# Transposed projections emitted in pieces of 12 matrix products instead of 6, in a two-layer hybrid attention encoder

## The chip, the cores and the metric

One Trainium2 chip, one core of it. The number is device time in microseconds (us) of one execution of the whole program, the median of several. Five engines of the core take part: PE (matrix products and transposes), DVE and POOL (elementwise), ACT (activation functions), SP (which here only issues DMAs). Each has its own list of instructions and goes through it in order; they meet through semaphores.

## The reference

Two layers over x of 512 positions by 1024 channels, float32. Each layer normalises x, multiplies it by one wide input matrix (1024 by 6152), runs three kinds of attention on the result, gates them, multiplies by one output matrix, normalises and adds:

```python
h = rms_norm(x, g_pre)
p = h @ w_in
qa, ka, va, ga, qs, ks, vs, gs, qf, kf, vf, gf, ff = jnp.split(p, split_at, axis=-1)
...
ya = diff_attention(qa, ka, va, lam, lambda_init, subln) * silu(ga)    # "a": 4 heads, two score maps each
yb = stick_breaking_attention(qs, ks, vs) * silu(gs)                    # "b": 8 heads
yc = forgetting_attention(qf, kf, vf, cum_log_f) * silu(gf)             # "c": 8 heads
y = jnp.concatenate([ya, yb, yc], axis=-1) @ w_out
return x + rms_norm(y, g_post)
```

(Reshapes between heads and channels are left out of this excerpt.) All three attentions are causal, and are taken in four blocks of 128 query positions; block i sees (i + 1) * 128 keys.

## The kernel before, in words

Full precision is made of three products: each operand is split in a high part and a rest (`hl`, `hT`), and `mm3` issues high by high (L192), high by rest (L193) and rest by high (L194) into one PSUM sum. A weight unit of 256 columns arrives by DMA, ACT copies its high part (L176) and POOL subtracts for the rest (L182).

There are two kinds of projections. `proj_N` makes v, with positions on the partitions. `proj_T` makes q, k and the gates transposed: 128 channels on the partitions, all 512 positions along the row, so that one projection is 8 chunks of the inner dimension times 3 products of 128x512, 24 in all. A layer has 36 of them (24 for q and k, 12 for the gates), the program 72.

Attention is woven between the projections by a list that the program sorts by a planned time. `do(cost, fn)` puts a piece of a projection on the main list and moves the planned clock `now` on by `cost`; `at(t, fn)` puts an operation of attention, or a copy out of PSUM, on the side list at a time t. In the end both lists are sorted together and emitted in that order. A piece of a projection is not divided: a side operation whose time falls within a piece is emitted behind it. The groups go a, c, b; the attention of a group runs while the next group's projections are on PE, and the attention of b while the gates are.

One step of attention (one head or one half of a pair, one block i) is a chain: scores on PE (L339, two products per score tile `s`), softmax pieces on DVE and ACT (L364 adds the mask and finds the minimum `mn`, L373 exponentiates, L464 and L466 normalise; in b, ACT takes two sigmoids at L499 and L500, and DVE scans and multiplies at L506 and L511), transposes on PE into `pt` (L347), a copy out of PSUM (L350 on ACT or L352 on DVE), and the product with v on PE (`ov`, L399 in a, L437 in b and c). The score tiles have two PSUM buffers, `pt` two, `ov` one, the projections `pj` three.

Of the kernel before, what the change touches and what calls it, by code (L numbers as in the profile page):

```python
# [60 lines left out]
def hybrid_kernel(ctx, tc, x, w_in, forget_bias, diff_lambda, diff_subln, w_out, pre_norm, post_norm, consts, out):  # L61
# [72 lines left out]
    def do(cost, fn):  # L134
        main.append((now[0], 1, len(main), fn))
        now[0] += cost

    def at(t, fn):
        side.append((t, 0, len(side), fn))
# [51 lines left out]
    def mm3(ps, lh, ll, rh, rl, first, last):  # L191
        nc.tensor.matmul(out=ps, lhsT=lh, rhs=rh, start=first, stop=False)  # L192
        nc.tensor.matmul(out=ps, lhsT=lh, rhs=rl, start=False, stop=False)  # L193
        nc.tensor.matmul(out=ps, lhsT=ll, rhs=rh, start=False, stop=last)  # L194

    def proj_T(k0, c, hT, done):

        st = {}

        def go(q):  # L200
            if q == 0:
                st["ps"] = pj_p.tile([128, S], F32, name="pj", tag="pj")
            for kc in range(2 * q, 2 * q + 2):
                w = halves[k0 + kc // 4]["hl"][:, :, kc % 4, c * 128:(c + 1) * 128]
                h = hT()
                mm3(st["ps"], w[:, 0], w[:, 1], h[0][:, kc], h[1][:, kc], kc == 0, kc == KC - 1)

        for q in range(4):
            do(1296, lambda q=q: go(q))
        for t, fn in done(st):  # L210
            at(now[0] + t, fn)

# [394 lines left out]
    def plan_layer(l, L):  # L607
# [9 lines left out]
        for g in ("a", "c", "b"):  # L617
# [44 lines left out]
            for u in range(2):  # L662
                for part in ("q", "k"):
                    k0 = add_in_unit(l, base + u * UW + (512 if part == "k" else 0))
                    use(k0, now[0])
                    use(k0 + 1, now[0] + 2600)
                    if g == "a" and u == 0 and part == "q":
                        for h in range(2):
                            halves[k0 + h].update(lead=2500, lo="both")
                    for cc in range(2):  # L670
                        keep = c["pairs"][2 * u + cc]
                        if part == "q":
                            proj_T(k0, cc, hT, lambda pst, keep=keep: qk_done(pst, g == "a", sc, keep, "q"))
                        else:
                            proj_T(k0, cc, hT, lambda pst, keep=keep: qk_done(pst, g == "a", 1.0, keep, "k"))
# [29 lines left out]
        for g in ("b", "a", "c"):  # L705
            ost = ctxs[g][0]
            for u in range(2):
                k0 = add_in_unit(l, G[g] + 1536 + u * UW)
                use(k0, now[0])
                use(k0 + 1, now[0] + 2600)  # L710
                for cc in range(2):
                    j = 2 * u + cc

                    def done(pst, g=g, j=j, ost=ost):
                        def times(a):
                            o = ost["o"]
                            nc.vector.tensor_tensor(out=o[:, j], in0=pst["ps"], in1=a, op=ALU.mult)

                        def sig(out):
                            nc.scalar.activation(out=out, in_=pst["ps"], func=AF.Sigmoid)  # L720

                        def gate():
                            pst["sg"] = t2("gs")
                            sig(pst["sg"])

                        if g == "b":
                            return [(0, gate), (1000, lambda: times(pst["sg"]))]
                        return [(300, lambda: times(ost["o"][:, j])), (800, lambda: sig(pst["ps"])),
                                (1700, lambda: times(ost["o"][:, j])), (2800, lambda: cut(g, j))]
                    proj_T(k0, cc, hT, done)  # L730
# [150 lines left out]
```

## Time and profile before

| | |
|---|---|
| median of 3 runs | 873.25 us (873.04 to 873.48) |
| the profiled execution | 873.66 us, of which the profile's span is 871.8 us |
| PE busy in the span | 854.9 us (98%), 4892 instructions |
| DVE, ACT, POOL busy | 495.3 us (57%), 476.9 us (55%), 449.6 us (52%) |
| granted TensorE clock, mean | 0.998 of 2.4 GHz |

The span runs from the first to the last instruction of the program; the rest of an execution's time lies around it. In the list of instructions in order of time, the first number is the start in us from the span's start, the second the time to the end of the last instruction that is merged in the row. Ends of matrix products are modelled and overlap, so starts are what to compare.

### The profile page before, as it was taken

What the parts mean: (1) busy time and instruction counts of PE and PEld (TensorE: products, weight loads), DVE (VectorE), ACT (ScalarE), POOL (GpSimd) and SP (SyncE); (2) the same over time, 40 slices, a digit from 0 to 9 for tenths busy, and PEclk for the clock granted to TensorE, in tenths of its full rate; (3) what the DMA queues carried; (4) which work ended last, traced back from release to release, by engine and by line L of the source; (5) the groups of instructions that cost most, each with busy time, mean ns of one, the idle gap of its engine ahead of it and who ended that gap; (6) DMA issues with size and microseconds to landing.
All of it is one profiled execution on the core that took longest, in us unless ns stands there. A gap on an engine that the chain in (4) does not pass through costs nothing.

```text
span 871.8 us, 13938 instructions
## 1 busy us (share of the span) xinstructions
PE 854.9 (98%) x4892; PEld 721.4 (83%) x4892; DVE 495.3 (57%) x1143; ACT 476.9 (55%) x1064; POOL 449.6 (52%) x680
## 2 busy tenths in 40 slices
PE   7999999999999999999999999999999999999997
PEld 5988998898778778777898889888987787877885
DVE  5378656544565778623563875664445476774322
ACT  4344667766776556633334356676667756664310
POOL 4366554655444548770364664555554544688301
PEclk9999999999999999999999999999999999999999
DMA  7365323432524221237264452325335422122522
GB/s 233 89 164 138 96 73 98 117 102 76 154 67 116 75 72 49 73 107 257 78 177 114 123 145 74 99 72 146 97 81 137 106 66 72 49 78 92 164 101 97
DMA packets 73207, 94.27 MB, mean 108 GB/s; under 512 B 6433, under 2 KB 56225, under 8 KB 73138
## 3 DMA queue, kind: packets, MB, share of 16 engines
q1 hardware_dynamic: 70834, 89.19, 35.6%
q10 hardware_dynamic: 2304, 4.20, 1.5%
q8 instruction: 39, 0.64, 0.3%
q14 instruction: 30, 0.25, 0.1%
HBM read 76.56 MB, written 4.23 MB: 93 GB/s over the span
## 4 chain that ended last, share of the span: by engine, by line
PE 78%; DVE 10%; ACT 4%; POOL 3%; issue 2%; DMA 2%; DVEq 0%; POOLq 0%; ACTq 0%; SPq 0%
PE pj L192 18%; PE pj L194 18%; PE pj L193 17%; PE s L339 6%; PE pt L347 5%; PE ov L437 4%; POOL hl L182 2%; PE acc L192 2%; PE acc L193 2%; PE acc L194 2%; PE ov L399 2%; DVE ra L307 2%; DVE sh L306 2%; DVE sh L303 1%; DVE qd L324 1%
## 5 line engine op out<-in xcount | busy, mean ns | idle before, releaser
L182 POOL TENSOR_TENSOR hl<-raw,hl 128x256 fp32r<-128x256 f32 (+1 forms) x420 | 343.5, 850 | 237.1 <-ACT hl L176 213.0
L192 PE MATMUL pj<-hT,hl 128*128 128x512 f32 x576 | 236.6, 411 | 0.0
L194 PE MATMUL pj<-hT,hl 128*128 128x512 f32 x576 | 225.7, 392 | 0.0
L193 PE MATMUL pj<-hT,hl 128*128 128x512 f32 x576 | 225.3, 391 | 0.0
L176 ACT ACTIVATE hl<-raw 128x1024 fp32r<-128x1024 f32 (+1 forms) x120 | 126.3, 1058 | 35.4 <-DMA raw<-in_w_out_dram 18.9
L194 PEld LDWEIGHTS pj<-hT,hl 128*128 128x128 f32 x576 | 108.1, 188 | 24.3
L192 PEld LDWEIGHTS pj<-hT,hl 128*128 128x128 f32 x576 | 108.4, 188 | 20.0 <-issue 2.1
L193 PEld LDWEIGHTS pj<-hT,hl 128*128 128x128 f32 x576 | 108.7, 189 | 16.9
L192 PE MATMUL pj<-hl,hT 128*128 128x256 f32 (+1 forms) x384 | 112.2, 292 | 0.3 <-ACT hT L257 0.2
L194 PE MATMUL pj<-hl,hT 128*128 128x256 f32 (+1 forms) x384 | 109.5, 285 | 0.5 <-DVE hT L258 0.5
L193 PE MATMUL pj<-hl,hT 128*128 128x256 f32 (+1 forms) x384 | 109.3, 285 | 0.5 <-POOL hl L182 0.5
L373 ACT ACTIVATE p<-p,mn 128x128 f32<-128x128 f32 (+3 forms) x128 | 71.1, 556 | 33.6 <-DVE mn L364 31.7
L506 DVE TENSOR_TENSOR_SCAN kp<-kp,c_masks 128x128 f32<-128x128 f32 (+3 forms) x64 | 67.2, 1051 | 18.3 <-ACT kp L499 17.8
L192 PEld LDWEIGHTS pj<-hl,hT 128*128 128x128 f32 x384 | 73.7, 192 | 1.3 <-ACT hT L257 1.0
L193 PEld LDWEIGHTS pj<-hl,hT 128*128 128x128 f32 x384 | 73.8, 192 | 1.2 <-POOL hl L182 0.7
L194 PEld LDWEIGHTS pj<-hl,hT 128*128 128x128 f32 x384 | 73.5, 191 | 1.2 <-DVE hT L258 1.2
L339 PE MATMUL s<-kd,qd 128*128 128x128 f32 (+1 forms) x192 | 62.6, 330 | 2.9 <-DVE mn L364 2.9
L350 ACT ACTIVATE pT<-pt 128x128 f32<-128x128 f32 (+3 forms) x96 | 41.2, 443 | 37.5 <-PE pt L347 37.2
L339 PE MATMUL s<-kd,qs 128*128 128x128 f32 (+1 forms) x192 | 61.2, 323 | 0.0
L511 DVE TENSOR_TENSOR sg<-sg,kp 128x127 f32<-128x127 f32 (+3 forms) x64 | 46.1, 721 | 5.5
L185 DVE TENSOR_TENSOR hl<-raw,hl 128x1024 fp32r<-128x1024 f32 (+2 forms) x18 | 21.0, 1175 | 44.8 <-ACT hl L176 44.7
L466 ACT ACTIVATE p<-p,rc 128x128 f32<-128x128 f32 (+3 forms) x64 | 35.0, 556 | 20.2 <-DVE rc L464 20.2
(142 smaller groups left out, 1453.0 us busy)
## 6 DMA issues: line engine op xcount, KB each, us to landing
raw<-in_w_in_dram SPq DMA_DIRECT2D x96, 512.0 KB, 3.7
qs<-qd SPq DMA_DIRECT2D x48, 256.0 KB, 4.5
raw<-in_w_out_dram SPq DMA_DIRECT2D x24, 512.0 KB, 3.6
cb<-cs ACTq DMA_DIRECT2D x16, 256.0 KB, 3.3
xl<-in_x_dram SPq DMA_DIRECT2D x4, 512.0 KB, 4.9
xt<-in_x_dram SPq DMA_DIRECT2D x8, 256.0 KB, 6.1
xs<-xt SPq DMA_DIRECT2D x8, 256.0 KB, 2.0
xt<-xs SPq DMA_DIRECT2D x8, 256.0 KB, 3.9
```

The costliest lines, as they stand in the source:

```text
L176: nc.scalar.activation(out=hl[:, 0], in_=raw, func=AF.Copy)
L182: nc.gpsimd.tensor_tensor(out=hl[:, 1, k, c:e], in0=raw[:, k, c:e], in1=hl[:, 0, k, c:e].bitcast(F32), op=ALU.subtract)
L192: nc.tensor.matmul(out=ps, lhsT=lh, rhs=rh, start=first, stop=False)
L193: nc.tensor.matmul(out=ps, lhsT=lh, rhs=rl, start=False, stop=False)
L194: nc.tensor.matmul(out=ps, lhsT=ll, rhs=rh, start=False, stop=last)
L339: nc.tensor.matmul(out=s[:, 0:n], lhsT=pr[q][:, m, i * 128:n], rhs=pr["k"][:, m, 0:n], start=(j == 0), stop=(j == 1))
L347: nc.tensor.transpose(out=pt[:, j * 128:(j + 1) * 128], in_=p[:, j * 128:(j + 1) * 128], identity=C["ident"])
L350: nc.scalar.activation(out=t, in_=src, func=AF.Copy)
L373: nc.scalar.activation(out=p[:, 0:n], in_=p[:, 0:n], func=AF.Exp, bias=st["mn", m], scale=-1.0, accum_out=su)
L466: nc.scalar.activation(out=p[:, 0:n], in_=p[:, 0:n], func=AF.Copy, scale=r)
L506: nc.vector.tensor_tensor_scan(out=rv, data0=rv, data1=C["first"][:, S - n:S][:, ::-1], initial=0.0, op0=ALU.mult, op1=ALU.max)
L511: nc.vector.tensor_tensor(out=sg[:, 0:n - 1], in0=sg[:, 0:n - 1], in1=kp[:, 1:n], op=ALU.mult)
```

## The change

`proj_T` is cut in two pieces of four chunks (12 products) instead of four pieces of two chunks (6 products); the planned cost of a piece is doubled with it, so that the planned clock after a projection is the same. Nothing else is changed. `proj_N` and the output projection keep their pieces.

```diff
         def go(q):
             if q == 0:
                 st["ps"] = pj_p.tile([128, S], F32, name="pj", tag="pj")
-            for kc in range(2 * q, 2 * q + 2):
+            for kc in range(4 * q, 4 * q + 4):
                 w = halves[k0 + kc // 4]["hl"][:, :, kc % 4, c * 128:(c + 1) * 128]
                 h = hT()
                 mm3(st["ps"], w[:, 0], w[:, 1], h[0][:, kc], h[1][:, kc], kc == 0, kc == KC - 1)
 
-        for q in range(4):
-            do(1296, lambda q=q: go(q))
+        for q in range(2):
+            do(2592, lambda q=q: go(q))
         for t, fn in done(st):
             at(now[0] + t, fn)
```

A side operation whose planned time falls in the first half of such a piece is now emitted up to one old piece (6 products) later among the products; one in the second half stays where it was. The lists of DVE, ACT, POOL and SP hold the same instructions in the same order as before. On PE the unbroken stretches of transposed products between operations of attention go from 192 to 110, by count of its list; 160 of the 192 were 6 products long, 100 of the 110 are 12.

Place A, in the PE list, while group c's attention (score pairs `s`, transposes `pt`) runs among b's projections (`pj`); before:

```order
L339 MATMUL s_2869<-kd_2124,qd_1941 128x256
L339 MATMUL s_2869<-kd_2124,qs_1956 128x256
L339 MATMUL s_2882<-kd_2124,qd_1941 128x256
L339 MATMUL s_2882<-kd_2124,qs_1956 128x256
L192 MATMUL pj_2802<-hT0_145,hl_2537 128x512
L193 MATMUL pj_2802<-hT1_146,hl_2537 128x512
L194 MATMUL pj_2802<-hT0_145,hl_2537 128x512
L192 MATMUL pj_2802<-hT0_145,hl_2537 128x512
L193 MATMUL pj_2802<-hT1_146,hl_2537 128x512
L194 MATMUL pj_2802<-hT0_145,hl_2537 128x512
L347 MATMUL pt_2906<-c_masks_134,p_2814 128x128
```

The same place with the change (the numbers of some tiles differ by 6, and `p_2820` is the `p_2814` of before):

```order
L339 MATMUL s_2875<-kd_2124,qd_1941 128x256
L339 MATMUL s_2875<-kd_2124,qs_1962 128x256
L339 MATMUL s_2888<-kd_2124,qd_1941 128x256
L339 MATMUL s_2888<-kd_2124,qs_1962 128x256
L347 MATMUL pt_2906<-c_masks_134,p_2820 128x128
```

The six products that stood between the second score pair and the transpose now stand ahead of the first pair.

Place B, some 10 us later on PE, still among c's attention; before:

```order
L347 MATMUL pt_2992<-c_masks_134,p_2885 128x128 x2
L339 MATMUL s_2999<-kd_2124,qd_1941 128x512
L339 MATMUL s_2999<-kd_2124,qs_1956 128x512
L192 MATMUL pj_2912<-hT0_145,hl_2791 128x512
L193 MATMUL pj_2912<-hT1_146,hl_2791 128x512
L194 MATMUL pj_2912<-hT0_145,hl_2791 128x512
L192 MATMUL pj_2912<-hT0_145,hl_2791 128x512
L193 MATMUL pj_2912<-hT1_146,hl_2791 128x512
L194 MATMUL pj_2912<-hT0_145,hl_2791 128x512
L339 MATMUL s_3013<-kd_2124,qd_1941 128x512
L339 MATMUL s_3013<-kd_2124,qs_1956 128x512
L347 MATMUL pt_3024<-c_masks_134,p_2922 128x128 x3
```

With the change:

```order
L347 MATMUL pt_2998<-c_masks_134,p_2891 128x128 x2
L339 MATMUL s_3005<-kd_2124,qd_1941 128x512
L339 MATMUL s_3005<-kd_2124,qs_1962 128x512
L339 MATMUL s_3013<-kd_2124,qd_1941 128x512
L339 MATMUL s_3013<-kd_2124,qs_1962 128x512
L347 MATMUL pt_3024<-c_masks_134,p_2928 128x128 x3
```

The two transposes and the first score pair have moved behind six more products. The transposes of that score's result (`pt_3091` in both lists) stand 12 products, three transposes, a score pair and a product with v behind `pt_3024`, as before.

Place D, on PE, while group b's attention runs among the gate projections; before:

```order
L339 MATMUL s_3655<-kd_3153,qs_2936 128x128
L347 MATMUL pt_3658<-c_masks_134,sg_3586 128x128 x4
L192 MATMUL pj_3648<-hT0_145,hl_3503 128x512
L193 MATMUL pj_3648<-hT1_146,hl_3503 128x512
L194 MATMUL pj_3648<-hT0_145,hl_3503 128x512
L192 MATMUL pj_3648<-hT0_145,hl_3503 128x512
L193 MATMUL pj_3648<-hT1_146,hl_3503 128x512
L194 MATMUL pj_3648<-hT0_145,hl_3503 128x512
L339 MATMUL s_3687<-kd_3153,qd_2909 128x256
L339 MATMUL s_3687<-kd_3153,qs_2936 128x256
L339 MATMUL s_3696<-kd_3153,qd_2909 128x256
L339 MATMUL s_3696<-kd_3153,qs_2936 128x256
```

With the change:

```order
L339 MATMUL s_3661<-kd_3153,qd_2909 128x128
L339 MATMUL s_3661<-kd_3153,qs_2942 128x128
L347 MATMUL pt_3664<-c_masks_134,sg_3592 128x128 x4
L339 MATMUL s_3687<-kd_3153,qd_2909 128x256
L339 MATMUL s_3687<-kd_3153,qs_2942 128x256
L339 MATMUL s_3696<-kd_3153,qd_2909 128x256
L339 MATMUL s_3696<-kd_3153,qs_2942 128x256
```

The six products between the first score pair's break and the two pairs after it now stand ahead of all three, so three score tiles follow each other without a product of a projection between them.

## Rows read from the trace of the kernel before

**Rows 1.** The page, part 1: busy time, share of the span, instructions.

```profile
PE 854.9 (98%) x4892; PEld 721.4 (83%) x4892; DVE 495.3 (57%) x1143; ACT 476.9 (55%) x1064; POOL 449.6 (52%) x680
```

**Rows 2.** PE's waits: line, what it waited for, total us, times, longest.

```profile
PE s L339 <- DVE mn L364: 2.9, 4, 1.1
...
PE pj L192 <- DVE y L756: 1.0, 1, 1.0
```

**Rows 3.** PE in order of time, 125.9 to 133.5 us: start, us, instruction.

```profile
125.92 0.48 PE L192 MATMUL pj<-hT,hl 128*128 128x512 f32 x1
...
128.74 0.22 PE L339 MATMUL s<-kd,qd 128*128 128x128 f32 x1
...
130.30 0.48 PE L192 MATMUL pj<-hT,hl 128*128 128x512 f32 x1
...
131.78 0.28 PE L339 MATMUL s<-kd,qd 128*128 128x256 f32 x1
...
132.02 0.40 PE L192 MATMUL pj<-hT,hl 128*128 128x512 f32 x1
...
133.41 0.28 PE L339 MATMUL s<-kd,qd 128*128 128x256 f32 x1
```

**Rows 4.** PE in order of time at place A (in brackets: idle before, releaser).

```profile
225.25 0.39 PE L339 MATMUL s<-kd,qd 128*128 128x256 f32 x1 [0.37 <-DVE mn L364]
...
225.60 0.40 PE L192 MATMUL pj<-hT,hl 128*128 128x512 f32 x1
...
226.97 0.27 PE L347 MATMUL pt<-c_masks,p 128*128 128x128 f32 x1
```

**Rows 5.** DVE in order of time at place A.

```profile
225.12 0.08 DVE L364 DVE_READ_ACCUMULATOR2_ANT mn<- 128x1 f32 x1
```

**Rows 6.** ACT in order of time at places A and B.

```profile
225.91 0.40 ACT L466 ACTIVATE p<-p,rc 128x128 f32<-128x128 f32 x1 [0.18 <-DVE rc L464]
...
237.13 0.49 ACT L350 ACTIVATE pT<-pt 128x384 f32<-128x384 f32 x1 [0.25 <-PE pt L347]
...
240.46 0.71 ACT L466 ACTIVATE p<-p,rc 128x512 f32<-128x512 f32 x1
```

**Rows 7.** PE in order of time at place B.

```profile
234.08 0.38 PE L347 MATMUL pt<-c_masks,p 128*128 128x128 f32 x2
...
241.22 0.66 PE L347 MATMUL pt<-c_masks,p 128*128 128x128 f32 x4
```

**Rows 8.** PE in order of time at places C and D.

```profile
272.27 0.27 PE L339 MATMUL s<-kd,qs 128*128 128x128 f32 x1
272.38 0.45 PE L192 MATMUL pj<-hT,hl 128*128 128x512 f32 x1
...
294.23 0.62 PE L347 MATMUL pt<-c_masks,sg 128*128 128x128 f32 x4
294.61 0.48 PE L192 MATMUL pj<-hT,hl 128*128 128x512 f32 x1
```

**Rows 9.** ACT in order of time at places C and D.

```profile
272.53 0.27 ACT L500 ACTIVATE sg<-s 128x127 f32<-128x127 f32 x1
...
294.89 0.60 ACT L350 ACTIVATE pT<-pt 128x512 f32<-128x512 f32 x1 [0.59 <-PE pt L347]
...
295.54 0.28 ACT L500 ACTIVATE sg<-s 128x127 f32<-128x127 f32 x1
```

**Rows 10.** PE in order of time at place E, group a's attention.

```profile
150.43 0.48 PE L192 MATMUL pj<-hT,hl 128*128 128x512 f32 x1
```

**Rows 11.** DVE in order of time at place E.

```profile
150.75 0.09 DVE L364 DVE_READ_ACCUMULATOR2_ANT mn<- 128x1 f32 x1
```

**Rows 12.** PE in order of time, second layer, the counterpart of place A.

```profile
652.17 0.38 PE L339 MATMUL s<-kd,qd 128*128 128x256 f32 x1 [0.37 <-DVE mn L364]
```

**Rows 13.** Busy us by engine in a stretch (PE, PEld, DVE, ACT, POOL), granted clock, DMA.

```profile
400.00:410.00 10.00, 9.02 (x40) 7.16 (x39) 3.71 (x5) 3.73 (x9) 0.76 (x4) 1.00 1.02 329
```

## The prediction

> **What bounds the kernel now.** I read the busy shares first: PE is at work 98% of the span, the other three little more than half [rows 1]. Nearly every us that leaves or enters PE's list therefore shows in the time, and an operation elsewhere matters only where PE has to wait for it. The list of PE's waits came next: they are few and short, scores that wait for a minimum on DVE (2.9 us over four times) and one product that waits 1.0 us for DVE's `y` [rows 2]. So attention's results are now in time almost everywhere on PE. The third view is PE's list in order of time. I looked there for two things: what a break between products costs in itself, and how early the result that each operation of attention needs has come. The second decides this change, since DVE, ACT, POOL and SP keep their lists and only PE's order moves.
>
> **What the change takes away: breaks.** A stretch of 12 products behind fp32 operations takes 128.74 - 125.92 = 2.82 us. One of 6 behind fp32 operations takes 131.78 - 130.30 = 1.48, and the one of 6 behind scores 133.41 - 132.02 = 1.39, together 2.87 [rows 3]. So where two stretches become one, at most 0.05 us goes; six products on their own run at 1.39 / 6 = 0.232 us each, a long stretch somewhat faster. At the least the gain is nothing, if the slower spacing belongs to the products' place and not to the break. I take 0.03 us, a little over the middle, since the slow spacing is met again at the start of the longer stretch. With 192 - 110 = 82 stretches fewer that is 82 x 0.03 = 2.5 us less (bounds 0 and 82 x 0.05 = 4.1). No product, transpose or DMA is added or removed.
>
> The Trainium skill (TensorE: Matmul & The Clock Gate, section Back-to-back issue gap) gives the isolated spacing of matmuls by their width alone, with no term for how many follow each other; for 512 columns it gives about 216 ns. By it this gain would be zero. The rows above show 0.232 us, so its figure does not hold here, and its rule is carried below as the second rival.
>
> **What it adds: waits.** Six products are 1.39 us. Between two operations of attention that depend on each other, they were the cover. Where they now stand ahead of both, PE reaches the second 1.39 us sooner after the first, and waits if the result between them was not that early. A PE that waits holds everything behind it in its list. From the end of a releasing instruction to the start on PE 0.05 us pass: the minimum ends at 225.12 + 0.08 = 225.20 [rows 5] and the score starts at 225.25 [rows 4]. I went through PE's new list and looked for places where the margin before was under 1.39 us. Five have none left, each once in a layer; the places in the first layer are:
>
> - A. Before, the transpose starts at 226.97, the six products ahead of it at 225.60 [rows 4]. The normalised `p` that it turns is ready at 225.91 + 0.40 = 226.31 on ACT [rows 6]. It now follows the second score pair, and that pair still waits for the same minimum, so PE is free for it at 225.60: wait 226.31 + 0.05 - 225.60 = 0.76 us.
> - B. From the two transposes at 234.08 to the four at 241.22 PE takes 7.14 us [rows 7], and the four start just when `p` is ready, 240.46 + 0.71 = 241.17 on ACT [rows 6]. They have no margin. Six of the products between leave, so PE is there after 7.14 - 1.39 = 5.75 us. The chain behind the first two transposes and the score beside them (copy, minimum, exponentials, normalising, on DVE and ACT) needs as long as before, except that ACT's 0.25 us for the transposes in between [rows 6] falls away: 6.89 us. Wait 1.14 us. The bounds are 1.39, if ACT gains nothing, and 0.5, if other idle time of ACT in that chain goes too.
> - C. Group b's two 128x128 score pairs are now followed at once by a third pair, which needs the first one's buffer; six products stood between. The second pair ends its turn on PE at 272.38 [rows 8], and the second sigmoid that reads the first pair ends at 272.53 + 0.27 = 272.80 on ACT [rows 9]: wait 272.85 - 272.38 = 0.47 us.
> - D. Behind the four transposes at 294.23 PE is free at 294.61 [rows 8]. One score pair fits in; with its start behind a break I take 0.35 us, as from 225.25 to 225.60 [rows 4]. The next needs the buffer of the pair ahead of the transposes, whose sigmoids stand on ACT behind the copy of those transposes (294.89, after a wait for PE) and end at 295.54 + 0.28 = 295.82 [rows 9]. Wait 295.87 - 294.61 - 0.35 = 0.91 us.
> - E. In group a a score pair follows two others and the transposes without the six products. PE is free at 150.43 [rows 10], one pair of 0.35 us is issued, and the minimum that empties the buffer ends at 150.75 + 0.09 = 150.84 [rows 11]: wait 150.89 - 150.78 = 0.11 us.
>
> A layer: 0.76 + 1.14 + 0.47 + 0.91 + 0.11 = 3.39 us. The second layer repeats the first: A's wait stands there with the same releaser and the same 0.37 us [rows 4, 12]. So 6.8 us are added. If DVE and ACT catch up during each wait, it may be 3.8 (1.9 a layer); if further places with little margin join, 8.1. Elsewhere the operations that move late or early keep their cover, because at least six, mostly 12 products stand ahead of the operation that needs them, and I cost them at nothing; were that cover gone, each would cost up to 1.39 us.
>
> For C and D the row shows a third score tile with two buffers and no other PE work between. The Trainium skill (Perfetto Trace Analysis, section Matmuls) says that independent matmul groups should rotate through PSUM banks, so that emptying one overlaps the products of the next; the change takes the overlapping products out from between. By that rule alone the sum would be the waits of C and D, 2 x (0.47 + 0.91) = 2.8 us, which the saved breaks would nearly pay. The rows say that A and B, which lack data and not a buffer, cost as much again.
>
> **Sum.** 6.8 - 2.5 = 4.3 us more. The profiled execution took 873.66 us (span 871.8 and 1.9 around it), 0.4 over the median of 873.25; from the median, 873.25 + 4.3 gives 877.6 us.
>
> **The rivals.**
> - Faster. The chains that PE would wait for end in time, because ACT and DVE idle some 45% of the span [rows 1] and run ahead; only the breaks count. Time 873.25 - 2.5 = 870.8. It decides at a wait of 1.25 us a layer: below that the kernel is faster. Against it speaks that at A to D the instruction in question starts only when PE has released it, so ACT's idle time lies ahead of the chain and not in it; B had no margin at all. 5%.
> - The waits as forecast, but no gain from longer stretches: 873.25 + 6.8 = 880.1. For it, the 0.05 us comes from three stretches with different neighbours. 15%.
> - The two nearly cancel, waits of 0.8 to 4.3 us against 2.5: within 0.2% (1.75 us, about what a measurement of this kernel can tell from no change). It would need A and B to shrink to a third. 9%.
> - More waits follow: an operation late on ACT holds the ones behind it, and places with margins of some tenths of a us join, three more a layer of 0.7 us: 873.25 + 4.3 + 4.2 = 881.8. 7%.
> - The clock. Waits of about 1 us could let PE's clock fall to 1.2 GHz. Against it, the stretch from 400 to 410 us, in which PE is idle for 0.98 us, has a granted clock of 1.00 [rows 13]. Ten us at the lower level would take some 9 us more of the 9.02 of PE's work: about 887. 2%. In the Trainium skill (TensorE: Matmul & The Clock Gate, section A second HAM failure mode) frequent short idling between groups of matmuls makes the clock go to and fro; the stretch just named does not show it.
>
> **Numbers.** The forecast itself holds 62%. It takes 877.6 us, with 875.2 to 880 as its own range. The range reaches to 881.4 above (the bound of 8.1 us of waits with no gain) and to 874.8 below (waits of 5.7 us, about halfway between their sum and their lower end, with the full 4.1 of gain); less than 2 in 10 is left out. Slower by over 0.2%: 62 + 15 + 7 + 2 = 86%; within: 9%; faster: 5%.
>
> **What would show it.** In the profile after, PE's busy time falls by up to some us while its waits grow from 2.9 for scores to several entries: `pt` L347 waiting for ACT's `p` L466 (A and B), `s` L339 waiting for ACT's `sg` L500 (C and D), each twice, 0.5 to 1.2 us long. Behind fewer breaks the second half of a 12-product stretch should show a spacing under 0.232 us. The prediction is wrong if those entries are missing or under 0.3 us, if other lines hold the larger waits, or if the granted clock is below 0.99.

## The result, and the profile after

With pieces of 12 the program takes 880.74 us (median of 4 runs, 880.67 to 882.67) against 873.30 us (4 runs) before: ratio 1.0091 (of the means, so that the one run of 882.67 us counts), 95% interval 1.0073 to 1.0108. By the medians that is 7.4 us slower. 877.6 us was forecast, with 874.8 to 881.4 as the range.

The profile of the changed kernel has a span of 878.8 us, 7.0 more than before. (The profiled execution of the kernel before took 873.66 us, 0.4 over its median; hence 7.0 here beside 7.4 above.) The granted clock is the same:

```profile
core 0: 878.8 us, clock 0.999
```

The page's part 1 of the changed kernel, to be held against [rows 1]:

```profile
PE 856.6 (97%) x4892; PEld 723.8 (82%) x4892; DVE 489.3 (56%) x1143; ACT 475.5 (54%) x1064; POOL 446.6 (51%) x680
```

The same number of instructions, and PE idle for 22.2 us of its span (878.8 - 856.6) instead of 16.9 (871.8 - 854.9). The other 1.7 us of the 7.0 stand in PE's busy time, which was forecast to fall. Busy time counts to modelled ends, and by the starts of the products, further down, the work did fall. What PE waits for is in the list of PE's waits (total us, times, longest), against [rows 2]:

```profile
PE pt L347 <- ACT p L466: 3.3, 4, 1.0
PE s L339 <- DVE mn L364: 3.0, 4, 1.1
...
PE s L339 <- ACT sg L500: 2.2, 4, 0.8
PE pj L192 <- DVE y L756: 0.8, 1, 0.8
...
PE acc L192 <- DVE oc L717: 0.4, 2, 0.2
```

The rest of the list of before, beside the two lines of [rows 2], holds neither ACT's `p` nor its `sg`:

```profile
PE pt L254 <- DVE xn L248: 2.5, 3, 1.3
PE s L582 <- DMA grow<-in_pre_norm_dram: 2.3, 1, 2.3
...
PE pj L194 <- DVE hT L258: 0.5, 2, 0.3
PE pj L193 <- POOL hl L182: 0.5, 1, 0.5
PE pj L192 <- ACT hT L257: 0.2, 1, 0.2
```

Two entries are new and large, and they are those that were named: transposes that wait for ACT's normalised `p` (four times: A and B in two layers), and scores that wait for ACT's sigmoids (four times: C and D in two layers). In the order of time on PE they stand where they were forecast; in brackets the idle time and its releaser:

```profile
226.98 0.38 PE L339 MATMUL s<-kd,qd 128*128 128x256 f32 x1 [0.45 <-DVE mn L364]
227.21 0.28 PE L339 MATMUL s<-kd,qs 128*128 128x256 f32 x1
228.09 0.33 PE L347 MATMUL pt<-c_masks,p 128*128 128x128 f32 x1 [0.61 <-ACT p L466]
...
241.91 0.39 PE L437 MATMUL ov<-pT,v 128*64 128x128 f32 x4
243.32 0.66 PE L347 MATMUL pt<-c_masks,p 128*128 128x128 f32 x4 [1.03 <-ACT p L466]
...
276.45 0.39 PE L339 MATMUL s<-kd,qd 128*128 128x256 f32 x1 [0.31 <-ACT sg L500]
...
299.94 0.38 PE L339 MATMUL s<-kd,qd 128*128 128x256 f32 x1 [0.79 <-ACT sg L500]
```

And their releasers in the order of time on ACT:

```profile
227.64 0.40 ACT L466 ACTIVATE p<-p,rc 128x128 f32<-128x128 f32 x1 [0.18 <-DVE rc L464]
...
242.56 0.70 ACT L466 ACTIVATE p<-p,rc 128x512 f32<-128x512 f32 x1
...
276.12 0.27 ACT L500 ACTIVATE sg<-s 128x127 f32<-128x127 f32 x1
...
299.60 0.28 ACT L500 ACTIVATE sg<-s 128x127 f32<-128x127 f32 x1
```

Each row of PE begins within 0.07 us of the end of its row on ACT: 227.64 + 0.40 = 228.04 and 228.09 at A, 243.26 and 243.32 at B, 276.39 and 276.45 at C, 299.88 and 299.94 at D. Before, the transpose at A started 0.66 us after its `p` was ready [rows 4, 6], and C and D had products ahead of them [rows 8].

The list of waits counts from modelled ends of products, and so too little. I also counted by starts: the distance from the start of each PE instruction to the start of the next, less the median distance of that pair of kinds in the kernel before, added up where it is over 0.11 us, past the first 25 us and leaving out the distances behind the first product of a chunk (L192) and between products of `ov`. That gives 6.6 us of waits before and 14.6 us after, 8.0 more; what is left of the span falls from 865.2 to 864.3 us, 0.9 less. Pairs that the kernel before does not have need another reference, and its choice moves these sums by some tenths of a us; they are estimates. By this count a wait is, in the first layer: A 0.77 us, B 1.10 (0.11 before), C 0.46, D 0.95, E 0.14; in the second layer each is within 0.01 us of that.

### The profile page after: what moved, and what is told of

It reads as the page before. It is cut to its first block, busy times and chain, and to the rows that moved or that the text cites. A ratio compares the mean times of both kernels' runs of the same rounds, so it can differ in the third digit from the quotient of the medians.

```text
span 878.8 us, 13934 instructions
## 1 busy us (share of the span) xinstructions
PE 856.6 (97%) x4892; PEld 723.8 (82%) x4892; DVE 489.3 (56%) x1143; ACT 475.5 (54%) x1064; POOL 446.6 (51%) x680
## 5 line engine op out<-in xcount | busy, mean ns | idle before, releaser
L192 PE MATMUL pj<-hT,hl 128*128 128x512 f32 x576 | 231.5, 402 | 0.0
L192 PEld LDWEIGHTS pj<-hT,hl 128*128 128x128 f32 x576 | 108.4, 188 | 21.1 <-issue 1.4
L192 PE MATMUL pj<-hl,hT 128*128 128x256 f32 (+1 forms) x384 | 112.7, 293 | 0.3 <-ACT hT L257 0.2
L192 PEld LDWEIGHTS pj<-hl,hT 128*128 128x128 f32 x384 | 74.0, 193 | 1.4 <-ACT hT L257 1.0
L339 PE MATMUL s<-kd,qd 128*128 128x128 f32 (+1 forms) x192 | 65.5, 345 | 5.2 <-DVE mn L364 3.0
L499 ACT ACTIVATE kp<-s 128x128 f32<-128x128 f32 (+3 forms) x64 | 28.4, 444 | 35.3 <-PE s L339 34.8
L511 DVE TENSOR_TENSOR sg<-sg,kp 128x127 f32<-128x127 f32 (+3 forms) x64 | 43.0, 672 | 5.8 <-DVE kp L506 0.5
```

The source lines that it names most:

```text
L339: nc.tensor.matmul(out=s[:, 0:n], lhsT=pr[q][:, m, i * 128:n], rhs=pr["k"][:, m, 0:n], start=(j == 0), stop=(j == 1))
L499: nc.scalar.activation(out=kp[:, 0:n], in_=s[:, 0:n], func=AF.Sigmoid, scale=-1.0)
L511: nc.vector.tensor_tensor(out=sg[:, 0:n - 1], in0=sg[:, 0:n - 1], in1=kp[:, 1:n], op=ALU.mult)
```

## The experiments

Two theories. **Cover**: the products between dependent operations of attention were what hid ACT's and DVE's work; where the longer pieces take them away, PE waits, at A to E and at few other places, and those waits are the whole loss. **Cost by itself**: longer pieces, or larger breaks, cost in proportion to the projections so cut, by whatever means. All times are medians, and each ratio is to the kernel before on the same chip. Its median is 873.01, 873.46 and 873.65 us on the three chips used here and 873.30 in the result above, so that a time is held against the change by how far each lies over its own kernel before; the change lies 7.4 us over.

### Where the pieces are long

For these four, `proj_T` takes the number of pieces as an argument, which each call gives:

```diff
-    def proj_T(k0, c, hT, done):
+    def proj_T(k0, c, hT, done, n=2):
...
-            for kc in range(2 * q, 2 * q + 2):
+            for kc in range(KC // n * q, KC // n * (q + 1)):
...
-        for q in range(4):
-            do(1296, lambda q=q: go(q))
+        for q in range(n):
+            do(5184 / n, lambda q=q: go(q))
```

**Pieces of 12 only in group b's q and k** (`n = 2 if g == "b" else 4`, gates 4).

> Pieces of 12 only in the q and k projections of group b (16 of the 72), 6 elsewhere. These run beside group c's attention and hold places A, B and C. Cover theory: the waits of A, B and C return in both layers, 2 x (0.77 + 0.99 + 0.46) = 4.4 us as the changed kernel's trace has them, less some 0.4 for 26 fewer stretches: about +4 us on the kernel before, 877.3. Rival (longer pieces cost by themselves, each the same): 16/72 of 7.4 us, +1.6, 874.9.

Measured: 878.42 us against 873.01, ratio 1.0061 (1.0044 to 1.0077): +5.4 us. A, B and C are there with the sizes of the change, D is not:

```profile
PE pt L347 <- ACT p L466: 3.3, 4, 1.0
PE s L339 <- DVE mn L364: 3.3, 4, 1.1
...
PE pj L192 <- DVE y L756: 1.6, 1, 1.6
PE s L339 <- ACT sg L500: 0.6, 2, 0.3
```

16 of the 72 projections make nearly three quarters of the loss, three times what cost by itself would give. The expectation of +4 lies within the interval. By starts the trace also shows what it left out: a longer wait for `y` (0.6 us more; in the lists of the kernels here it is between 0.2 and 1.6 us, where it stands), A's old wait for the minimum (0.4 us more), and two small waits a layer beside A and B (0.15 and 0.12 us), which the change has too.

**Pieces of 12 only in the gates** (`n = 2` there, 4 elsewhere).

> Pieces of 12 only in the gate projections (24 of the 72), beside group b's attention; place D. Cover theory: 2 x 0.95 = 1.9 us of waits, less 0.5 for 34 fewer stretches: +1.4, 874.7; A, B and C as in the kernel before. Rival (cost by itself): 24/72 of 7.4, +2.5, 875.8.

Measured: 875.05 us against 873.01, ratio 1.0024 (1.0014 to 1.0033): +2.0 us, between the two expectations, and by the time alone undecided. The profile decides it: the only large new entry in PE's waits is D's, once a layer (0.95 us each by starts). Of the small ones, `hl` on POOL and `oc` on DVE have 0.4 us more each than before, and `y` 0.8 us less.

```profile
PE s L339 <- DVE mn L364: 2.9, 4, 1.1
...
PE s L339 <- ACT sg L500: 1.6, 2, 0.8
PE pj L193 <- POOL hl L182: 0.9, 2, 0.5
...
PE acc L192 <- DVE oc L717: 0.4, 2, 0.2
...
PE pj L192 <- DVE y L756: 0.2, 1, 0.2
```

**Pieces of 12 only in groups a's and c's q and k** (`n = 4 if g == "b" else 2`, gates 4).

> Pieces of 12 only in the q and k projections of groups a and c (32 of the 72); beside c's runs group a's attention, beside a's none. Place E and one small wait near it. Cover theory: 2 x (0.14 + 0.28) = 0.8 us of waits, less 0.3 for 22 fewer stretches: +0.5, 873.8, no difference that can be told. Rival (cost by itself): 32/72 of 7.4, +3.3, 876.6.

Measured: 873.88 us against 873.01, ratio 1.0009 (0.9999 to 1.0018): +0.9 us, as cover has it within the interval, and far from +3.3: 32 of the 72 projections cost next to nothing when the attention beside them keeps its cover. The three parts together make 5.4 + 2.0 + 0.9 = 8.3 us against 7.4 for the whole change, a difference that the intervals allow.

**Pieces of 3** (`n = 8` everywhere).

> Pieces of 3 products everywhere (264 stretches instead of 192). Cover theory: operations of attention come nearer to their planned times and in smaller breaks, so no wait is added; the kernel before's small waits at A (0.53 us a layer) may go. Breaks cost 72 times 0.015 to 0.03 us, 1.1 to 2.2 us. Together 872.5 to 875. Rival (fewer and larger breaks are what pays, 0.05 us each): 72 x 0.05 = 3.6 us, 877.

Measured: 872.82 us against 873.01, ratio 0.9994 (0.9985 to 1.0004): no difference. PE's list of waits has the scores' wait for the minimum twice instead of four times (the wait at A is gone):

```profile
PE s L339 <- DVE mn L364: 2.1, 2, 1.1
```

By starts the waits fall from 6.6 to 5.6 us, and the rest of the span grows from 865.2 to 865.8 us: 0.6 us for 72 more stretches, about 0.01 us each. The rival's 877 is out.

### The cover given back

These four change planned times, on pieces of 12 unless the last.

**Group c's transposes 1296 ns later.**

```diff
-            at(d + 4261, lambda m=m: turn(m))
+            at(d + 5557, lambda m=m: turn(m))
```

> Pieces of 12 everywhere, and the transposes of group c's attention planned 1296 ns (six products) later, so that A and B have their cover again. Cover theory: both waits vanish in both layers, 2 x (0.77 + 0.99) = 3.5 us less than the change: 877.2; C, D and E stay. Rival (the wait moves on to the product with v or to the next use of the two transpose buffers): no better than 880.

Measured: 876.16 us against 873.46, ratio 1.0032 (1.0019 to 1.0044): 2.7 us over the kernel before, 4.7 less than the change instead of 3.5 (3.7 less by the spans of the two profiles, 878.8 and 875.1). The entry for `p` has left PE's list of waits; C and D are as they were:

```profile
PE s L339 <- DVE mn L364: 2.8, 2, 1.7
...
PE s L339 <- ACT sg L500: 2.2, 4, 0.8
```

The wait has not moved on to another line. What is gained beyond A and B are small waits in their train (0.15 and 0.12 us a layer by starts) and part of the old wait for the minimum at A (0.61 us by starts in the change, 0.3 to 0.4 here, by the reference taken). One wait outside the changed stages is 0.66 us longer here (1.9 us by starts, for a minimum in group a of the second layer). The profiled execution took 877.18 us, 1.0 over the median, so this wait may belong to that execution; what causes it is not shown. It has the same length in the profile of the first version in between, further down, and 1.2 us by starts in those of the others with both shifts.

**The second query block of group b's steps 1296 ns later.**

```diff
-        n = (i + 1) * 128
+        n, t = (i + 1) * 128, t + (1296 if i == 1 else 0)
```

> Pieces of 12 everywhere, and the second of the four query blocks of each step of group b planned 1296 ns later, so that its score pairs no longer follow two others at once. Cover theory: C and D vanish, 2 x (0.46 + 0.95) = 2.8 us less than the change: 877.9; A, B and E stay. Rival (the third score tile only meets the next break): no better than 880.

Measured: 877.44 us against 873.46, ratio 1.0047 (1.0034 to 1.006): 4.0 us over the kernel before, 3.5 less than the change instead of 2.8 (3.0 less by the spans, 878.8 and 875.8). Here the entry for the sigmoids has gone, and A and B stay:

```profile
PE pt L347 <- ACT p L466: 3.3, 4, 1.0
PE s L339 <- DVE mn L364: 3.0, 4, 1.1
```

**Both shifts, pieces of 12.**

> Pieces of 12 with both shifts. Cover theory: 3.5 and 2.8 us add up, 874.4 at most; if the shifts also take the waits that stood in the kernel before at A and the small ones of the change, down to 870. Rival (longer pieces cost by themselves): 7 us above the next kernel.

Measured: 873.36 us against 873.46, ratio 0.9997 (0.9989 to 1.0006). The loss is gone with the two entries, though every piece is 12 products long. 870 is not reached: E and a transpose near it, 0.14 and 0.27 us a layer, and 0.3 to 0.4 us at A's old wait stay.

```profile
PE s L339 <- DVE mn L364: 2.1, 2, 1.1
PE pj L192 <- DVE y L756: 0.7, 1, 0.7
```

**Both shifts, pieces of 6**, the control.

> Pieces of 6, as before, with both shifts (176 stretches; with pieces of 12 it is 108). It is the control of the kernel with both shifts: what is left between the two is the price of 68 breaks and of the remaining waits. Cover theory: 1.3 us under the kernel before, about 872 (A's old wait goes), and 1 to 2 us above the pieces of 12 with both shifts if those are free of waits. Rival: no change against before, 873.3.

Measured: 873.28 us against 873.46, ratio 0.9998 (0.9989 to 1.0007). The 872 expected of it did not show: the time is that of its rival, no change. Yet its waits are 1.2 us less by starts than before, and its profiled span is 871.0 us against 871.8. About half of the 1.2 us is the wait for `y`, which differs from kernel to kernel as said above. And the profiled execution lies 0.4 us under its median here (872.84 against 873.28), and 0.4 over it in the kernel before; that makes up the 0.8 us between the spans. Against the kernel with pieces of 12 and both shifts there is no difference in time: 1.4 us fewer waits, and 0.8 us more for the rest of the span (865.6 against 864.8) with 176 stretches instead of 108, about 0.01 us each. Cost by itself, which had 7 us between the two, is refuted.

### Buffer or data

**Three score buffers, two for projections, pieces of 12.**

```diff
-    pj_p = P("pj", 3, space=PS)
-    s_p = P("s", 2, space=PS)
+    pj_p = P("pj", 2, space=PS)
+    s_p = P("s", 3, space=PS)
...
-                            acc[tt] = (pj_p if tt < 3 else s_p).tile([128, S], F32, name="acc",
-                                                                    tag="pj" if tt < 3 else "s")
+                            acc[tt] = (pj_p if tt < 2 else s_p).tile([128, S], F32, name="acc",
+                                                                    tag="pj" if tt < 2 else "s")
```

> Pieces of 12 as in the change, with three PSUM buffers for score tiles and two instead of three for projections (the first output half then sums in two of each). If C and D are waits for the buffer of a score tile, all four entries of scores that wait for the sigmoids vanish (2.2 us in the list of waits of the changed kernel, 2.8 us by starts). A and B lack data, not a buffer, and stay: transposes waiting for normalised p, 3.3 us. Rival (C and D lack something else, such as ACT's turn): the entries stay. The two projection buffers will add waits of their own, so the time is compared with the next kernel, not with the change: 2 x (0.77 + 0.99) = 3.5 us more than it, less about 0.9 for the breaks.

**The same buffers, pieces of 6.**

> Control of the kernel with three score buffers: the same buffers with pieces of 6. It shows what two projection buffers cost, 1 to 3 us more than the kernel before; no scores waiting for sigmoids and no transposes waiting for p.

Measured: 882.70 us with pieces of 12, 876.89 with pieces of 6, against 873.65 for the kernel before; ratios 1.0099 (1.0086 to 1.0113) and 1.0035 (1.0021 to 1.0048). PE's waits with pieces of 12:

```profile
PE pt L347 <- ACT p L466: 4.7, 4, 1.3
PE pj L192 <- DVE ra L305: 3.2, 2, 1.9
...
PE acc L192 <- DVE oc L717: 1.8, 2, 0.9
```

and with pieces of 6:

```profile
PE pj L192 <- DVE ra L305: 2.6, 2, 1.3
...
PE acc L192 <- DVE oc L717: 1.5, 2, 0.8
PE pj L192 <- DVE ff L654: 0.9, 2, 0.5
```

No score waits for a sigmoid in either: C and D were waits for the buffer of a score tile. E and A's old wait for the minimum are gone too by starts, so those were of the same kind. The transposes' wait for `p` stays with pieces of 12, so A and B lack data. It has grown (4.7 us instead of 3.3), since a score no longer stops PE ahead of A's transpose and all of the waiting falls on the transpose:

```profile
229.51 0.33 PE L347 MATMUL pt<-c_masks,p 128*128 128x128 f32 x1 [1.32 <-ACT p L466]
```

The difference of the two, 5.8 us, is twice the 2.6 expected: A's transpose takes 1.48 us by starts instead of 0.77, and other transposes in group a wait 0.5 us a layer that did not before. With pieces of 6 the other buffers cost 3.2 us in all (1 to 3 were expected); the largest new entry is line L192's wait for DVE's rotation `ra`, 2.6 us.

### A version in between

**Both shifts; 12 for b's q and k and the gates, 6 for groups a and c.**

> Both shifts, pieces of 12 for group b's q and k and the gates, 6 for groups a and c. Beside group a's attention the change added 0.14 + 0.28 us of waits a layer (E and a transpose near it); without them, and with some 22 breaks more at 0.011 us, 0.8 - 0.2 = 0.6 us under the kernel with both shifts: 872.8.

Measured: 872.81 us against 873.65, ratio 0.9992 (0.9983 to 1.0001).

**Both shifts; 3 for a's and c's q and k, 6 for b's, 12 for the gates.**

> Both shifts; pieces of 3 beside groups a's attention (q and k of a and c), 6 for group b's q and k, 12 for the gates. Each stage has the piece that left it the fewest waits; 0.6 us a layer of waits remain less than with 12 everywhere. 872 to 873, at best 0.15% under the kernel before.

Measured: 873.30 us against 873.65, ratio 0.9992 (0.9983 to 1.0001). Neither can be told from the kernel before; no version here is shown to beat it.

## Why the prediction was right, and where sizes were off

The mechanism and the places were right, and each wait came out near its working: A 0.77 us by starts (0.76 was worked out), B 1.10 - 0.11 = 0.99 (1.14), C 0.46 (0.47), D 0.95 (0.91), E 0.14 (0.11). A layer makes 3.31 us where 3.39 stood in the sum. That the two kinds (A and B, C and D) are separate causes is shown by the two shifts, each of which takes away its own entry alone, and by the third score buffer, which takes away C and D (with E and A's old wait for the minimum) and leaves A and B.

The size is another matter. 880.74 us lies above the forecast's own range of 875.2 to 880, and 0.6 us from the rival that has no gain from longer stretches (880.1), where the forecast is 3.1 us away. The wide range held because its upper end, 881.4, allowed for further waits and for no gain together, and for the first of these the prediction gave no working; that the sum of the two came out so near the bound is luck.

Two terms were mis-sized, both in the direction of too small a loss.

- **The gain from fewer breaks**: 0.03 us was taken per stretch, 2.5 us for 82. The rest of the span fell by 0.9 us, about 0.01 each, as much as the pieces of 3 and the pair of kernels with both shifts give. The step that failed is the reading of [rows 3], which takes one stretch of each kind for all. The stretch of 12, 2.82 us, is the shortest of its 14 in the kernel before (behind other work than scores), whose mean is 2.853. The means of the two kinds of 6 are 1.481 (96 behind other work) and 1.396 (60 behind scores). So 0.024 us are between them, not 0.05, and the middle of that bound is 0.01. In the order of time on PE, a stretch of 12 in the changed kernel shows what is really won:

```profile
228.18 0.48 PE L192 MATMUL pj<-hT,hl 128*128 128x512 f32 x1
228.50 0.39 PE L193 MATMUL pj<-hT,hl 128*128 128x512 f32 x1
...
229.65 0.39 PE L192 MATMUL pj<-hT,hl 128*128 128x512 f32 x1
...
230.79 0.39 PE L194 MATMUL pj<-hT,hl 128*128 128x512 f32 x1
```

  From the second product to the seventh it takes 1.15 / 5 = 0.230 us each, from the seventh to the twelfth 1.14 / 5 = 0.228. Over all 100 stretches of 12 in that trace the means are 0.2306 and 0.2279 us. Six products gain about 0.01 us by standing second.
- **Other waits**: "costed at nothing" were the places outside A to E. By starts they add 0.29 us (a transpose at 156.5 us, behind a product with v in group a), 0.15 (a product with v at 231.9), 0.12 (the second of two sets of transposes at 265), 0.14 (the first product of the output sum at 378.6) and 0.08 (A's old wait), 0.78 us in the first layer and nearly the same in the second; the single wait for `y` is 0.2 us shorter. The reason for costing them at nothing, that at least six products stand ahead of the operation in need, did not hold at the largest: before, six products ran from 154.56 us between the products with v and these transposes, and with the change they stand ahead of both, the same loss of cover as at A. All waits together came to the bound that was named (8.1 us; 8.0 came).

So 8.0 - 0.9 = 7.1 us in the profiled span (7.0 by the spans themselves; 7.4 by the medians, as said above), where 6.8 - 2.5 = 4.3 was forecast. Of the signs that were named, one failed: PE's busy time rose by 1.7 us, because a part of the waits stands in it by the modelled ends (A to D are 3.28 us a layer by starts and 2.74 by the rows in brackets). The rivals: that the chains would end in time anyway is refuted by the two entries; that the breaks are worth nothing was nearly so, and with further waits beside it makes the measured time; that more waits follow came true with five places a layer, but with 0.78 us and not three times 0.7; the clock stayed where it was, with a granted 1.00 also in a stretch that holds three of the longer waits (650 to 680 us, 2.1 us idle):

```profile
650.00:680.00 30.00, 27.92 (x161) 22.36 (x160) 16.30 (x69) 21.27 (x49) 14.67 (x27) 1.00 0.52 140
```

The rule of the Trainium skill (Perfetto Trace Analysis, section Matmuls) that independent groups should rotate through banks was borne out at C and D, as the third buffer shows; it says nothing of A and B, which cost more. The isolated spacing in the Trainium skill (TensorE: Matmul & The Clock Gate, section Back-to-back issue gap) goes by the width alone, about 216 ns for 512 columns, and has no term for the length of a run. With 0.01 us per run that is close to right as to the length; the spacing itself is 0.228 to 0.232 us here. For a sustained stream of 512 columns the same section of the Trainium skill gives 131 ns. No run here shows that: in a stretch of 144 products the spacing is 0.227 us.

What stays open: which waits outside the changed stages, that for `y` above all, differ from kernel to kernel and which from execution to execution (there is one profile of each kernel), and with it whether the pieces of 6 with both shifts really have fewer waits than the kernel before.

## What to carry to other kernels

Where one engine is the bound and goes through its list in order, the work between two dependent operations on it is the cover of everything that the other engines do between them. Before making pieces larger, measure for each such pair how much earlier its input was ready than its start; where the margin is less than the work that moves away, the difference is the price. Here a break cost about 0.01 us and a lost piece of cover up to 1.1 us, so the size of the pieces had to follow the dependences, and moving two planned times by one old piece gave all the loss back.

## What was not expected of the hardware

A break in a run of 128x512 products, with transposes or scores put in between, costs PE only about 0.01 us beyond the work put in. Three different pairs of kernels say so, each with 0.6 to 0.9 us between two profiles. A straight line through the same count for all twelve kernels that have the buffers of before (106 to 264 stretches) rises by 0.009 us a stretch; single kernels lie up to 0.4 us off it, so one pair alone would not settle it.
